# A third pair of feed-forward blocks by seven products of halves, with six weight pieces halved by DMA

## The chip, the cores and the metric

The program runs on one core of one Trainium2 chip. TensorE (PE; its weight loads are PEld) multiplies, VectorE (DVE) and ScalarE (ACT) do elementwise work, GpSimd (POOL) and SyncE (SP) issue DMAs here, and POOL computes a few small things besides. The metric is the device time of one execution in microseconds, as the median of several runs.

## The reference

Two layers on 512 tokens of 1024 channels, in fp32: a Griffin RG-LRU block, a feed-forward block (FFN), an RWKV-7 block, a second FFN, and a final RMSNorm. What matters here is the FFN, which is computed once per layer:

```
def _conv_ffn(x, norm, w_up, conv_w, conv_b, w_down):
    h = _rmsnorm(x, norm)
    u = jnp.einsum('btd,df->btf', h, w_up)
    gate = _causal_dwconv(u[..., :D_FF], conv_w, conv_b)
    hid = jax.nn.gelu(gate, approximate=True) * u[..., D_FF:]
    return jnp.einsum('btf,fd->btd', hid, w_down)
```

`D_FF` is 3072, so `w_up` is 1024 x 6144 and `w_down` 3072 x 1024; the causal convolution runs over three tokens.

## The kernel before, in words

**Precision by halves.** Every fp32 operand of a large product is written as a sum of two parts in the type that the profile calls fp32r: the rounded value (high half) and what is left (low half). `mm3` (line 81 is its matmul) issues three matmuls for one product: high x high, high x low, low x high.

**Pieces of weights.** All weights lie in DRAM as pieces of 128 x 1024 fp32 (512 KB). `plan_weights` writes their order down once, as a list. `weights_load(upto)` issues the loads of the list up to a place, `weights_split(upto)` makes the halves: ACT copies the piece into the high half (line 123), DVE subtracts (line 127). `next_weights(ahead)` loads and splits some pieces ahead of the one that it hands out. Pieces in the set `self.rounded` go another way: a DMA on POOL's queue casts the piece straight from DRAM into the high half (line 201), ACT writes its negative (line 228), and a second DMA on POOL's queue adds the piece from DRAM to that (line 229). So DVE does nothing for such a piece, and DRAM is read twice. In the kernel before these are 12 pieces of the RWKV block. All other plain loads are on SP's queue (line 206).

**The pool of buffers.** Raw pieces, halves, the normalized input `xs` and its copies `xm` share one pool of 24 buffers of 4 KB per partition (tag `b4`, `N4 = 24`). A buffer that is not free holds up the load or the copy that wants it. A planner orders each engine's instructions: it takes, in program order, what is ready by its own cost estimates, so a split or a load may stand well ahead of the place in the code that asks for it. Inside one engine the order is then fixed.

**The FFN.** The 24 blocks of 128 gate channels and 24 blocks of 128 up channels are taken as 12 pairs `n` (two gate blocks and two up blocks each). There are two ways to compute a pair:

- `Whole`: four pieces, named G0, U0, G1, U1 (gate or up, first or second 512 input channels), each 24 matmuls of 512 columns. After G1, DVE scales the gate into `gpad`, and `gate` makes convolution (ACT line 733, DVE line 735) and gelu (ACT line 736). After U1, DVE and ACT make the hidden block and its halves.
- `Halves`: input channels, tokens and gate/up are each cut in two, and the 2 x 2 products are made with seven products instead of eight, in Strassen's manner. Each product is 24 matmuls of 256 columns. They are numbered and ordered `(1, 2, 6, 5, 7), (3, 4)`, with accumulators A, D, A, F, A, F, A. Five pieces are loaded, named by the product that they first serve (f5, f1, f2, f7, f4); f5 and f7 get a second piece added by a DMA on POOL's queue (line 213). The weights of product 6 are f1 + f5, summed by DVE (line 782). Those of product 3 are that sum plus another piece, added by a POOL DMA (line 799) once the halves of product 6 are made. The halves of all seven are made by ACT and DVE on line 789. Products 1, 6 and 7 are copied out by ACT (line 817); DVE adds the rest (lines 825 to 837).

In the kernel before, pairs 0, 1 and 2 are `Whole` and pairs 3 to 11 are `Halves` (`HALVES = range(3, 12)`). The sequence of the first three pairs holds only products up; between products 7 and 3 of every later pair, and after its product 4, stands one piece of the product down, 24 matmuls of 512 columns.

**What the halves need first.** `operands()` forms the summed inputs of products 4 to 7 (tiles `xt`): 16 scaled sums and 16 low halves on DVE (lines 658 to 673), and copies on ACT. The generator `moved()`, stepped by `next(moving)`, copies parts of `xs` into `xm` with 24 ACT copies (line 693), after which products 1, 2 and 3 read `xm`; six of the 24 matmuls of product 1 go on reading `xs`. Its four steps copy 4, 4, 8 and 8 parts.

**Looking ahead in the FFN.** `products(upto, more)` goes through the sequence of (pair, product). Before each product it asks `ahead` for the weights of the next `more` products. `weights(p)` of a `Halves` pair makes the halves; for a `Whole` pair `next_weights` does it.

**The norm.** While pair 0 runs, PE makes the sums of squares (`ssq`, after G0) and later spreads the inverse root over the partitions (`rbc`, line 376, after U0); between them POOL raises to the power -0.5 (`rs`, line 372). In the second layer PE also transposes `x` into token order between the pieces of pairs 0 and 1 (`xtk`, line 627).

Of the kernel before, what the change touches and what calls it, by code (L numbers as in the profile page):

```python
# [27 lines left out]
N4 = 24  # L28
WARM = 23

HALVES = range(3, 12)

PARAMS = [
    [("lru_b_in", 16), ("lru_conv_w", 32), ("lru_conv_b", 8),
# [10 lines left out]
def pieces():  # L45

    def full(name, lead, groups):
        for g in groups:
            for k in range(0, 8, 2):
                yield name, lead, k * P, g * 512, 2  # L50

    yield from full("lru_w_in", (0,), [2, 3, 0, 1])
    yield from full("lru_w_out", (0,), [0, 1])
    for i in (1, 0):
        yield from full("rwkv_w_rkv", (0, i), [0, 1])
    for g in range(4):
        for k in range(0, 8, 4):
            yield "rwkv_w_rkv", (0, 2), k * P, g * 256, 4
    for h in range(2):
        for g in range(4):  # L60
            yield "rwkv_w_out", (0,), h * 512, g * 256, 4
    for l in range(2):
        for n in range(12):
            for j in range(2):
                for i in range(2):
                    yield "ffn_w_up", (l,), j * 512, (1 - i) * DFF + n * 256, 4
        for k in range(0, FB, 2):
            for g in range(2):
                yield "ffn_w_down", (l,), k * P, g * 512, 2


class Kernel:
# [62 lines left out]
    def plan_weights(self):  # L135
        I = self.I
        plan = []
        self.quads = {}

        index = {key: i for i, key in enumerate(pieces())}  # L140

        def piece(w, r0, c0, k):
            return I["weights"][index[w + (r0, c0, k)]].rearrange("p (k c) -> p k c", k=k)

        def add(w, r0, c0, k=2):
            plan.append((piece(w, r0, c0, k), k, False, None))

        def full(w, groups, rows=8):
            for g in groups:
                for k in range(0, rows, 2):  # L150
                    add(w, k * P, g * 512)

        def ffn(l):
            up, dn = ("ffn_w_up", (l,)), ("ffn_w_down", (l,))

            def gu(n):
                self.quads[l, n] = len(plan)
                a = lambda i, j: piece(up, j * 512, (1 - i) * DFF + n * 256, 4)
                if n in HALVES:
                    for first, more in (((1, 1), (1, 0)), ((0, 0), None), ((0, 1), None), ((1, 0), (0, 0)), ((1, 1), None)):  # L160
                        plan.append((a(*first), 4, True, more and a(*more)))
                else:
                    for i, j in ((1, 0), (0, 0), (1, 1), (0, 1)):
                        plan.append((a(i, j), 4, False, None))

            def dd(row, n, groups):
                for g in groups:
                    for k in range(0, n, 2):
                        add(dn, row + k * P, g * 512)

            for n in range(12):
                gu(n)
                if 3 <= n < 11:
                    dd((n - 3) // 2 * 512, 4, ((n - 3) % 2,))
            dd(2048, 8, (0, 1))

        full(("lru_w_in", (0,)), [2, 3, 0, 1])
        full(("lru_w_out", (0,)), [0, 1])
        ffn(0)
        r0 = len(plan) + 8  # L180
        for i in (1, 0):
            full(("rwkv_w_rkv", (0, i)), [0, 1])
        for g in range(4):
            for k in range(0, 8, 4):
                add(("rwkv_w_rkv", (0, 2)), k * P, g * 256, 4)
        self.rounded = range(r0, r0 + 12)
        for h in range(2):
            for g in range(4):
                add(("rwkv_w_out", (0,)), h * 512, g * 256, 4)
        ffn(1)  # L190
        self.plan = plan
        self.loaded, self.splitted = {}, {}
        self.n_load = self.n_split = self.n_used = 0
# [49 lines left out]
    def next_weights(self, ahead=2):  # L243
        while self.plan[self.n_used][2]:
            self.n_used += 1
        i = self.n_used
        self.weights_load(i + (3 if ahead < 3 else ahead + 2))
        self.weights_split(i + ahead)
        self.n_used += 1
        return self.splitted.pop(i)  # L250
# [355 lines left out]
    def ffn(self, l, xs, finish, after=None):  # L606
        nc, tc = self.nc, self.tc
        last = l == 1
        with tc.tile_pool(name=f"ffn{l}", bufs=1) as pool:
# [21 lines left out]
            def start(c):  # L631
                if c == 0:
                    norm.append(self.norm_end(rbs))
                    next(norm[0])
                elif c == 1:
                    next(norm[0])
                    if last:
                        self.push(by_tokens())
# [208 lines left out]
            quads = [self.quads[l, n] for n in range(12)]  # L847
            pairs, hids = {}, []
            kind = lambda n: Halves if n in HALVES else Whole
            seq = [(n, p) for n in range(12) for part in kind(n).order for p in part]  # L850
            made, at, cap = [0], [0], [len(seq)]

            def ahead(j):
                while made[0] < min(j, cap[0]):
                    n, p = seq[made[0]]
                    if n not in pairs:
                        pairs[n] = kind(n)(n)
                    pairs[n].weights(p)
                    made[0] += 1

            def products(upto, more=2):

                while True:
                    n, p = seq[at[0]]
                    at[0] += 1
                    ahead(at[0] + more)
                    pairs[n].product(p)
                    if p == "G0" and n == 2:
                        self.weights_load(quads[n + 1] + 4)
                    if n == 0 and p in ("G0", "U0"):  # L870
                        start(int(p == "U0"))
                    if n == 1 and p == "U0":
                        op.update(operands())
                    if (n, p) in ((1, "G1"), (1, "U1"), (2, "U0"), (2, "G1")):
                        next(moving)
                    if p == 5:
                        self.weights_split(quads[n] + 7)
                    if (n, p) == upto:
                        return
# [56 lines left out]
            def room(b):  # L936
                if b % 2 == 0:
                    rooms.append(pool.tile([P, 2, 2, T], F32R, tag="xt", name="hx", bufs=4))
                return rooms[-1][:, b % 2, 0], rooms[-1][:, b % 2, 1]

            products((2, "U1"))
            for n in range(3, 12):
                cap[0] = seq.index((n, 7)) + 1
                products((n, 7))
                cap[0] = seq.index((n, 4)) + 1
                ahead(at[0] + 2)
                if n < 11:
                    self.weights_load(quads[n + 1] + 2)

                def between():  # L950
                    cap[0] = len(seq)
                    if n < 11:
                        self.weights_load(quads[n + 1] + 4)
                    products((n, 4))
                    if n < 11:
                        ahead(at[0] + 3)
                        held.append(pairs[n + 1].sum)
                    elif not last:
                        self.push(self.lora_weights())

                if n < 11:
                    down((n - 3) % 2, (n - 3) // 2 * 4, 4, between)
                    ahead(at[0] + 2)
                    continue
                if not last:
                    self.norm_begin()
                down(0, 16, 8, between)
                down(1, 16, 8)
# [110 lines left out]
    @staticmethod  # L1079
    def bytok(t):  # L1080
        return t.rearrange("p (c q t) -> p c q t", q=2, t=C)
# [127 lines left out]
    def rwkv_krv(self, pool, mk, mr, AR, BK, PC, selk, LTs):  # L1209
# [95 lines left out]
        def ev_r(b, ps):  # L1305
            self.need(("r", b))
            rr = self.outer(AR, b)
            nc.vector.tensor_tensor(rr, bytok(ps), rr, ALU.mult)

        def trail(i, out, counts):  # L1310
            gen = self.mixes(i, out)
            return lambda c: [next(gen, None) for _ in range(counts[c])]

        self.push(prepare(0))
        mv = []
        self.project(mk, lambda o, ps: nc.scalar.copy(self.outer(BK, 4 + o), bytok(ps)), after=trail(0, mr, (0, 0, 2, 2)), rate=1.2, ahead=3)
        self.push(prepare(1))
        self.push(self.solve(0, AR, BK, LTs), 1)
        self.project(mr, lambda o, ps: ev_r(o, ps), rate=0.4, rate1=1.2, ahead=3)
        self.project(mr, lambda o, ps: ev_r(4 + o, ps), after=trail(2, mv, (4, 2, 2, 2)), rate=1.3, rate1=0.9, ahead=3)  # L1320
        self.tasks[0].extend(self.tasks[1])
        self.tasks[1].clear()
        return mv
# [568 lines left out]
```

## Time and profile before

| | |
|---|---|
| median of 3 runs | 1250.02 us (1249.42 to 1250.54) |
| the profiled execution | 1250.2 us, span 1248.5 us, granted clock 0.997 |
| PE busy | 1225.5 us, 98% of the span |
| DVE, ACT, POOL busy | 963.7, 678.8, 147.7 us |
| first FFN, pairs 0 to 2 | from 153.2 to 220.4 us |
| second FFN, pairs 0 to 2 | from 867.2 to 938.2 us |

Times in rows of the profile are in us from the start of the span. In the rows of a timeline or of the chain the first number is the start, the second the duration; `x24` means that 24 instructions were merged into the row; a bracket gives the idle time before and what ended it. In rows by line, the numbers after the bar are the busy time of the group in us and the mean of one in ns. Matmuls overlap in the pipeline, so the pitch from one row's start to the next is what a product costs, not the duration of one matmul.

### The profile page before, as it was taken

To read this page: it belongs to the slowest core of one execution; us is meant where nothing else is said; L and a number is where in the kernel's file an instruction comes from. 1 tells how busy PE (TensorE), PEld (TensorE's weight loads), DVE (VectorE), ACT (ScalarE), POOL (GpSimd) and SP (SyncE) were. 2 spreads that over 40 slices of the span, in tenths; PEclk is the share of its full clock that TensorE was granted. 3 is DMA by queue.
4 is the path that set the end of the run, shared out by engine and by line. 5 is a ranking of instruction groups with operands and counts; after the bars stand their busy time and mean duration, and the time that the engine had idled before them with its cause. 6 is when DMAs were issued, how large, how long until landed. Compare 5 with 4: busy or idle time off the path is not lost.

```text
span 1248.5 us, 23681 instructions
## 1 busy us (share of the span) xinstructions
PE 1225.5 (98%) x9795; PEld 1068.2 (86%) x9795; DVE 963.7 (77%) x1453; ACT 678.8 (54%) x1074; POOL 147.7 (12%) x234
## 2 busy tenths in 40 slices
PE   9999999999999999999999998999999999999997
PEld 7777888999999998878679887778889999999986
DVE  7988686777777776989898957678766777777764
ACT  6697465444444444668755356445754444444442
POOL 0000000000100000020233145310000001000000
PEclk9999999999999999999999999999999999999999
DMA  6322233666666664511566122022337666666631
GB/s 261 102 68 85 96 100 92 181 174 170 169 173 177 176 199 143 177 59 62 113 155 164 36 64 87 29 86 86 101 85 186 170 169 169 173 175 178 197 122 69
DMA packets 49389, 164.60 MB, mean 132 GB/s; under 512 B 6304, under 2 KB 8608, under 8 KB 49152
## 3 DMA queue, kind: packets, MB, share of 16 engines
q1 hardware_dynamic: 37040, 120.08, 28.1%
q0 software_dynamic: 11376, 41.42, 17.6%
q8 instruction: 77, 1.26, 0.4%
q10 hardware_dynamic: 864, 1.57, 0.4%
q14 instruction: 32, 0.26, 0.1%
HBM read 158.53 MB, written 4.52 MB: 131 GB/s over the span
## 4 chain that ended last, share of the span: by engine, by line
PE 43%; DVE 5%; ACT 3%; issue 1%; POOL 0%; POOLq 0%; DVEq 0%; ACTq 0%
PE accA L81 8%; PE acc L81 5%; PE accF L81 4%; PE acc L908 3%; PE acc L907 3%; PE acc L909 3%; PE accU L81 3%; PE accG L81 3%; PE accD L81 2%; DVE X L1391 1%; PE s L1505 1%; DVE DA L1389 1%; PE acc L1337 1%; PE pe L1549 1%; PE pd L1587 1%
## 5 line engine op out<-in xcount | busy, mean ns | idle before, releaser
L789 DVE TENSOR_TENSOR lo<-raw,hi 128x1024 fp32r<-128x1024 f32 x126 | 152.2, 1219 | 27.6 <-ACT hi L789 13.3
L127 DVE TENSOR_TENSOR wl<-raw,wh 128x1024 fp32r<-128x1024 f32 (+1 forms) x117 | 140.7, 1210 | 28.5 <-ACT wh L123 25.4
L81 PE MATMUL accA<-xt,hi 128*128 128x256 f32 x864 | 149.8, 276 | 0.0
L789 ACT CAST hi<-raw 128x1024 fp32r<-128x1024 f32 x126 | 129.4, 1047 | 34.0 <-PE acc L908 12.6
L81 PEld LDWEIGHTS accA<-xt,hi 128*128 128x128 f32 x864 | 130.2, 188 | 0.0
L123 ACT CAST wh<-raw 128x1024 fp32r<-128x1024 f32 (+1 forms) x116 | 119.2, 1044 | 18.7 <-PE accU L81 6.9
L81 PE MATMUL accA<-xt,lo 128*128 128x256 f32 x432 | 119.3, 276 | 0.0
L81 PE MATMUL acc<-hid,wh 128*128 128x512 f32 x384 | 118.2, 390 | 0.0
L817 ACT COPY s<-accA 128x512 f32<-128x512 f32 x54 | 31.7, 588 | 144.4 <-PE accA L81 144.4
L733 ACT ACTIVATE cv<-gpad,pv 128x512 f32<-128x512 f32 x48 | 37.2, 811 | 96.6 <-DVE gpad L837 93.2
L81 PEld LDWEIGHTS acc<-hid,wh 128*128 128x128 f32 x384 | 70.2, 188 | 13.1
L81 PEld LDWEIGHTS accA<-xt,lo 128*128 128x128 f32 x432 | 81.2, 188 | 0.0
L81 PE MATMUL acc<-xs,wh 128*128 128x512 f32 x248 | 77.8, 395 | 1.1 <-ACT wh L123 1.1
L213 POOL DMA_DIRECT2D raw<-in_weights_dram x36 | 31.6, 877 | 383.6 <-DMA raw<-in_weights_dram 267.6
L908 PE MATMUL acc<-wh,hid 128*128 128x512 f32 (+1 forms) x200 | 76.3, 381 | 0.0
L907 PE MATMUL acc<-wh,hid 128*128 128x512 f32 (+1 forms) x200 | 76.2, 381 | 0.0
L909 PE MATMUL acc<-wl,hid 128*128 128x512 f32 (+1 forms) x200 | 76.2, 381 | 0.0
L81 PE MATMUL acc<-hid,wl 128*128 128x512 f32 x192 | 74.5, 390 | 0.0
L735 DVE SCALAR_TENSOR_TENSOR cv<-gpad,pv,cv 128x512 f32<-128x512 f32 x96 | 67.2, 747 | 4.4 <-ACT cv L733 4.3
L81 PE MATMUL accU<-xs,wh 128*128 128x512 f32 x192 | 59.8, 392 | 0.0
L81 PE MATMUL accG<-xs,wh 128*128 128x512 f32 x192 | 59.7, 392 | 0.0
L81 PE MATMUL acc<-mix,wh 128*128 128x512 f32 x192 | 59.7, 392 | 0.0
(387 smaller groups left out, 3206.6 us busy)
## 6 DMA issues: line engine op xcount, KB each, us to landing
raw<-in_weights_dram SPq DMA_DIRECT2D x205, 512.0 KB, 4.4
raw<-in_weights_dram POOLq DMA_DIRECT2D x54, 512.0 KB, 5.6
wh<-in_weights_dram POOLq DMA_DIRECT2D x12, 512.0 KB, 6.5
wl<-in_weights_dram POOLq DMA_DIRECT2D x12, 512.0 KB, 7.0
xd<-x SPq DMA_DIRECT2D x8, 256.0 KB, 2.1
AR<-xd SPq DMA_DIRECT2D x1, 2048.0 KB, 8.6
x<-in_xT_dram SPq DMA_DIRECT2D x3, 512.0 KB, 7.0
out_dram<-xtok ACTq DMA_DIRECT2D x4, 256.0 KB, 2.1
```

The costliest lines, as they stand in the source:

```text
L81: mm = lambda *a, **kw: self.nc.tensor.matmul(ps, *a, skip_group_check=more, **kw)
L123: put = (self.nc.vector.tensor_copy if dve else self.nc.scalar.copy)(hi, src)
L127: rest = self.nc.vector.tensor_tensor(lo, src, hi.bitcast(F32), ALU.subtract)
L213: self.nc.gpsimd.dma_start(raw, more, accum_op=ALU.add)
L733: nc.scalar.activation(cv, pair.gp[:, e, 0:T], AF.Identity, bias=self.vec(f"ffn_conv_b{l}", fb), scale=cw(0))
L735: nc.vector.scalar_tensor_tensor(cv, pair.gp[:, e, j : j + T], cw(j), cv, ALU.mult, ALU.add)
L789: pair.at[p] = nc.scalar.copy(hi, f[p]), tt(lo, f[p], hi.bitcast(F32), ALU.subtract)
L817: copied = nc.scalar.copy(s[p], bank["A"])
L907: nc.tensor.matmul(ps, hh[:, s], wh[:, k, m], start=kk == 0, stop=False)
L908: nc.tensor.matmul(ps, hl[:, s], wh[:, k, m], start=False, stop=False)
L909: nc.tensor.matmul(ps, hh[:, s], wl[:, k, m], start=False, stop=kk == blocks - 1)
L1337: nc.tensor.matmul(ps, hh[:, s], wh[:, k, :], start=kk + b % 2 == 0, stop=False)
```

## The change

Pair 2 becomes a `Halves` pair too (`HALVES = range(2, 12)`). It has no piece of the product down between its products. In each layer the pieces G1 and U1 of pair 0 and all four of pair 1 join the set `self.rounded`. `next_weights` looks one piece further ahead where such a piece is near. The call of `operands()` moves from after U0 to after G0 of pair 1. The four steps of `moved()` move from pairs 1 and 2 (`Whole`) to after the products 1, 2, 3 and 4 of pair 2. The first loads of a `Halves` pair are asked for after G0 of pair 1 (for pair 2) and after product 7 of pair 2 (for pair 3). The argument `ahead=3` goes from two projections whose pieces are all in the set and so get 3 in `next_weights`.

```
-HALVES = range(3, 12)
+HALVES = range(2, 12)
...
-        self.rounded = range(r0, r0 + 12)
+        self.rounded = set(range(r0, r0 + 12))
...
         ffn(1)
+        for l in range(2):
+            self.rounded.update(range(self.quads[l, 0] + 2, self.quads[l, 2]))
...
         i = self.n_used
+        if i + 2 in self.rounded:
+            ahead = max(ahead, 3)
         self.weights_load(i + (3 if ahead < 3 else ahead + 2))
...
                     pairs[n].product(p)
-                    if p == "G0" and n == 2:
+                    if p == "G0" and n == 1:
                         self.weights_load(quads[n + 1] + 4)
...
-                    if n == 1 and p == "U0":
+                    if n == 1 and p == "G0":
                         op.update(operands())
-                    if (n, p) in ((1, "G1"), (1, "U1"), (2, "U0"), (2, "G1")):
+                    if (n, p) in ((2, 1), (2, 2), (2, 3), (2, 4)):
                         next(moving)
...
-            products((2, "U1"))
+            products((1, "U1"))
+            products((2, 7))
+            self.weights_load(quads[3] + 4)
+            products((2, 4))
+            ahead(at[0] + 2)
             for n in range(3, 12):
...
-        self.project(mr, lambda o, ps: ev_r(o, ps), rate=0.4, rate1=1.2, ahead=3)
-        self.project(mr, lambda o, ps: ev_r(4 + o, ps), after=trail(2, mv, (4, 2, 2, 2)), rate=1.3, rate1=0.9, ahead=3)
+        self.project(mr, lambda o, ps: ev_r(o, ps), rate=0.4, rate1=1.2)
+        self.project(mr, lambda o, ps: ev_r(4 + o, ps), after=trail(2, mv, (4, 2, 2, 2)), rate=1.3, rate1=0.9)
```

## The prediction, made before the run

> **What bounds the kernel now.** I read the page first, then the chain of waits in order of time, then stretches of the two FFNs.
>
> ```profile
> span 1248.5 us, 23681 instructions
> PE 1225.5 (98%) x9795; PEld 1068.2 (86%) x9795; DVE 963.7 (77%) x1453; ACT 678.8 (54%) x1074; POOL 147.7 (12%) x234
> PE 43%; DVE 5%; ACT 3%; issue 1%; POOL 0%; POOLq 0%; DVEq 0%; ACTq 0%
> ```
>
> ```profile
> 932.93 5.44 PE accU L81 x24
> 938.37 2.77 PE accA L81 x24
> 941.14 2.72 PE accD L81 x24
> 943.86 2.72 PE accA L81 x24
> 946.58 2.72 PE accF L81 x24
> 949.30 2.72 PE accA L81 x24
> 957.48 2.83 PE accF L81 x24
> 960.30 2.83 PE accA L81 x24
> 968.57 2.77 PE accA L81 x24
> ```
>
> The chain passes here through PE alone, each piece starting where the last ends: a `Whole` piece takes 5.44 us, a product of halves 2.72 to 2.83. Between 949.30 + 2.72 and 957.48 runs the piece down (5.46 us), which stands between products 7 and 3; another stands after product 4.
>
> ```profile
> 153.20:220.40 67.20, 67.20 (x306) 55.88 (x305) 51.36 (x86) 41.10 (x77) 3.88 (x3) 1.00 0.36 102
> 867.20:938.20 71.00, 71.00 (x337) 58.94 (x337) 50.69 (x84) 46.10 (x87) 3.75 (x3) 1.00 0.32 89
> 250.50:280.60 30.10, 30.10 (x218) 28.14 (x217) 22.93 (x30) 13.50 (x19) 2.61 (x3) 1.00 0.66 175
> 600.00:640.00 40.00, 37.67 (x279) 29.23 (x279) 36.00 (x71) 27.38 (x55) 11.30 (x14) 1.00 0.69 159
> ```
>
> In these rows of stretches stand length, then busy us of PE, PEld, DVE, ACT, POOL, the clock, the share of the DMA engines, GB/s. Pairs 0 to 2 (first two rows) have PE busy throughout and DVE 76 and 71%; a later pair (third row) has PE full and DVE 76%. So PE is the bound in both FFNs. Whatever shortens its stream is gained in full, unless a new wait opens.
>
> **The change, part by part.** *Pair 2.* A `Whole` pair is 4 x 5.44 = 21.76 us. Seven products are 2.77 + 4 x 2.72 + 2 x 2.83 = 19.31 if pair 2 is like the first pair of halves above, with pair 3 unchanged. Gain: 2.45 us a layer, 4.9 in both. If pair 2 takes over the slow places of products 3 and 4, and pair 3 gets 2.72 in their stead, it is 2.67 a layer, 5.3 in both.
>
> ```profile
> L81 PE MATMUL accA<-xs,hi 128*128 128x256 f32 x72 | 13.6, 282 | 0.0
> L81 PE MATMUL accA<-xm,hi 128*128 128x256 f32 x216 | 38.0, 277 | 0.0
> L123 ACT CAST wh<-raw 128x1024 fp32r<-128x1024 f32 x115 | 118.6, 1048 | 18.1 <-PE accU L81 6.9 <-PE acc L81 5.1 <-DMA raw<-in_weights_dram 4.4
> L228 ACT ACTIVATE wl<-wh 128x1024 fp32r<-128x1024 f32 x12 | 12.3, 1053 | 0.2
> L789 DVE TENSOR_TENSOR lo<-raw,hi 128x1024 fp32r<-128x1024 f32 x126 | 152.2, 1219 | 27.6 <-ACT hi L789 13.3 <-PE accU L81 12.7 <-PE acc L81 0.8
> L735 DVE SCALAR_TENSOR_TENSOR cv<-gpad,pv,cv 128x512 f32<-128x512 f32 x96 | 67.2, 747 | 4.4 <-ACT cv L733 4.3
> L830 DVE TENSOR_TENSOR s<-s,accF 128x512 f32<-128x512 f32 x18 | 12.4, 688 | 52.2 <-ACT s L817 52.2
> L693 ACT CAST xm<-xs 128x256 fp32r<-128x256 f32 x48 | 16.5, 402 | 5.4 <-PE accG L81 4.1 <-DVE wl L127 0.7 <-PE accU L81 0.4
> ```
>
> *Where pair 2 reads.* Its products 1, 2 and 3 run before the steps of `moved()`, so 66 more matmuls a layer read `xs` instead of `xm`. Product 1, with six matmuls on `xs`, is 0.05 us over product 2: 8 ns each, 0.53 a layer; the means by line differ by 5 ns. Between 0 and 0.53 I take 0.3: 0.6 in both. So PE's work falls by about 4.3 us. What is left are waits.
>
> *DVE and ACT.* Six subtractions of 1.22 us (7.3) leave DVE; ACT's six copies of 1.05 become six negations of the same length. Pair 2 costs DVE seven subtractions and a sum (9.8), four of line 735 (3.0) and some eleven of 0.69 (7.6): 20.3 us, against 4.9 + 3.0 + 8 x 0.69 = 13.4 for a `Whole` pair. So DVE's total hardly changes (+6.9 - 7.3), but 20.3 us now stand inside 19.3 us of PE. ACT gets seven copies for four, and the 24 copies of `moved()` (9.7 us) fall inside pair 2; in the first two stretches it has 25 us free.
>
> *The rounded pieces.* SP loses six loads of plain kind a layer, POOL gains twelve.
>
> ```profile
> raw<-in_weights_dram SPq DMA_DIRECT2D x205, 512.0 KB, 4.4
> L229 POOL DMA_DIRECT2D wl<-in_weights_dram x12: 866/899/1588, 597.3 to 665.6; - x12
> DMA to landing us min/median/max: 5.3/7.0/12.6
> PE rec L1289 <- DVE n L1285: 1.7, 2, 1.5
> 155.63 4.83 ACT L123 CAST wh<-raw 128x1024 fp32r<-128x1024 f32 x5
> 159.84 1.94 POOL L372 TENSOR_TENSOR rs<-ms,mhalf 128x4 f32<-128x4 f32 x1 [132.42 <-DVE ms L366]
> 165.01 1.05 PE L376 MATMUL rbc<-ident,rs 128*128 128x128 f32 x8
> 165.81 0.71 PE L81 MATMUL accG<-xs,wh 128*128 128x512 f32 x2
> ```
>
> The second and third rows are the adding DMA of the 12 pieces rounded already: 0.9 us of POOL's time, landing after 5.3 to 12.6. PE's waits from 580 to 700 us, where those are used, have no DMA among them (the fourth row is the longest). The tightest place is the first such piece, G1 of pair 0. ACT's five copies stand at 155.63; the first is U0's, the second G1's, so its negation ends near 157.6. Landing then comes at 163 to 170, by the median at 164.7; G1 starts at 165.81 and needs its low half 0.46 us later. Wait: 0 to 4 us a layer; nothing is to be won, since PE has no gap there. I take 0.2, near the median. Behind that wait on PE stand all later pieces, so each us counts. POOL's power (line 372) now has up to three issues ahead of it, 2.7 us; PE wants it at 165.01 and it ends at 161.78, so 3.2 us cover it and I cost it at nothing. Without the cover it costs what it is late. Pair 2's own first loads, asked for after G0 of pair 1, put two more additions on POOL, each held until its raw piece lands (4.4 us); behind them may stand the additions for pair 1's last pieces, which PE wants two or three pieces (10.9 to 16.3 us) later, so that is covered.
>
> The Trainium skill, "DMA: Bandwidth & Descriptors", section "Anatomy of one DMA", puts a POOL DMA at 2.0 us plus its bytes over 436 GB/s, an estimate of 3.2 us here. By that the wait above could not arise, and my first rival's chance would fall to nearly nothing; the 7.0 of the trace decides against it.
>
> *The earlier sums.* `operands()` must be done before product 6.
>
> ```profile
> 177.62 0.48 DVE L667 SCALAR_TENSOR_TENSOR s<-x,pv,s 128x256 f32<-128x256 f32 x1
> 193.35 0.75 DVE L658 TENSOR_TENSOR xt<-s,xt 128x256 fp32r<-128x256 f32 x2
> ...
> 209.03 1.23 DVE L789 TENSOR_TENSOR lo<-raw,hi 128x1024 fp32r<-128x1024 f32 x1 [5.84 <-PE accU L81]
> ```
>
> Its DVE work runs from 177.62 to 194.1 in the first layer. It is asked for one piece (5.44 us) earlier now and meets fewer subtractions, so it should end between 188 and 194. Pair 2 starts near 198.6 (one `Whole` pair before 220.33, below) and its product 6 near 204.1. Before that DVE has the evacuation of pair 1 (3.0 + 8 x 0.69 = 8.5) and two subtractions, the sum and a third (4.9): 13.4 us in 10 to 16. Late by 0 to 3.4; I take 0.1. DVE's idle 5.84 us before 209.03 are at pair 2 itself, so work can be drawn forward there.
>
> *The weights of product 3.* Here the piece down is missing as cover.
>
> ```profile
> 220.33 0.40 PE L81 MATMUL accA<-xs,hi 128*128 128x256 f32 x2
> 222.12 1.23 DVE L789 TENSOR_TENSOR lo<-raw,hi 128x1024 fp32r<-128x1024 f32 x1
> 223.64 0.87 POOL L799 DMA_DIRECT2D raw<-in_weights_dram  x1 [24.67 <-DVE lo L789]
> DMA to landing us min/median/max: 5.2/5.5/8.6
> ```
>
> In pair 3 now, product 1 starts at 220.33, the halves of product 6 end at 223.35, and POOL issues the addition at 223.64. With 5.2 to 8.6 us to land (the last row, all 18 of line 799) and 1.05 + 1.22 for the halves, product 3 could start 10.8 to 14.2 us after product 1. It is due there after 957.48 - 938.37 = 19.11 us now, in pair 2 after 2.77 + 4 x 2.72 = 13.65. So a slack of at least 4.9 falls to between 2.8 and -0.6, and DVE being late adds to it. A wait of 0 to 0.6; I take 0.2 a layer, since most of the 18 land near 5.5.
>
> *The turn to pair 3.* Its loads are asked for after product 7 of pair 2, 5.5 us before pair 3 instead of three whole pieces. SP gets four issues there; the two additions on POOL wait for their raw pieces (4.4 us), with the addition for pair 3's product 3 behind them. DVE has the gate of pair 2 (3.0 + 4 x 0.69) in the same us as pair 3's first splits. Nobody needs that gate before the piece down after pair 3's product 7, so it can slide; I take 0.1 a layer, between 0 and the 5.44 of the missing piece. The removed `ahead=3` changes no instruction: those pieces get 3 from the set.
>
> *Sum.* -4.9 + 0.6 + 2 x (0.2 + 0.1 + 0.2 + 0.1) = -3.1. The profiled execution of 1250.2 us (1.7 over its span) gives 1247.1; the median 1250.02 is 0.2 lower, so 1246.9.
>
> **The rivals.** *No change: late landings.* If the additions for G1 land after 10 us instead of 7, PE waits about 1.4 us a layer there, and with them the largest wait above, 0.6, at product 3: 4.0 in all, and 1249.9. For it: several POOL DMAs stand close together, as in the stretch from 600 us, where the DMA share is 0.69 and the longest landing 12.6. Against it: no wait of PE on a DMA there.
>
> *Slower: DVE becomes the bound.* From the start of `operands()` at 177.62 to pair 3's product 6, near 223.4, DVE has 45.8 us. It has 3.4 left of pair 0 (five of 0.69), 13.6 of sums (16 of 0.48, 16 of 0.37), 8.5 of pair 1, 20.3 of pair 2 and 4.9 of pair 3's first splits: 50.7. Unless the sums start earlier or the gate of pair 2 (5.8) slides, PE waits 4.9 us a layer. Price at 4 a layer: -4.3 + 8 = +3.7, 1253.9. It decides for slower by over 0.2% from 3.4 a layer. Against it: the idle DVE time before 209.03 and the earlier start, which together are worth more than 4.9.
>
> *Slower still: POOL starved.* If POOL could issue only while DVE rests, 24% of the first stretch, 0.9 us would become 3.7, and two issues a piece 7.5 where PE takes 5.44: 2.1 us x 6 a layer, 25 in both, 1271. The 0.9 us stand where DVE is busy 36.00 of 40 us, which would make them 9; that speaks against it. The Trainium skill, "SBUF — State Buffer", section "SBUF: two separate sides", has this rule: VectorE in a two-port mode locks GpSimd out of writing descriptors. By that row the trace does not agree for this kernel's subtractions.
>
> **How the numbers follow.** About 0.2%, 2.5 us, is what a measurement of this kernel can tell from no change. Forecast, losses under 2: 0.55, at 1244.7 to 1247.5. Late landings: 0.27, 1247.5 to 1252.5. DVE bound: 0.16, 1252.5 to 1256. POOL starved: 0.02. Faster 0.55, same 0.27, slower 0.18. The range from 1244.6 to 1252.6 leaves out the last two.
>
> **What would show it.** PE rows of 2.72 to 2.83 for seven products at pair 2 in both layers, close on one another; G1 of pair 0 starting right behind `rbc`; no waits of PE on `wl`, `lo` or a DMA between pair 0 and pair 3. The prediction is wrong if PE's gaps in that stretch exceed 2.4 us in all, or if matmuls on `xs` cost more than 8 ns extra.

## The result and the profile after

| | before | after |
|---|---|---|
| median, runs taken together | 1249.64 us (1248.76 to 1250.54) | 1257.85 us (1256.76 to 1259.55) |
| ratio, 95% interval | | 1.0069 [1.0059, 1.0079] |
| the profiled execution | 1250.2 us, span 1248.5 | 1256.76 us, span 1255.1 |

The change costs 8.2 us by the medians. A gain of 3.1 was forecast, and the range ended at 1252.6. The profiled executions are 6.6 us apart, since after's is the shortest of its six and before's is over its median. From after's page, span and busy time:

```profile
span 1255.1 us, 24039 instructions
PE 1223.2 (97%) x9939; PEld 1071.7 (85%) x9939; DVE 961.5 (77%) x1455; ACT 685.5 (55%) x1086; POOL 170.8 (14%) x264
```

PE has 2.3 us less to do than the 1225.5 of before, and the span is 6.6 longer: the loss is waiting. Lines after 190 of the kernel stand 2 to 8 further down in after than in before. The three longest lines of PE's waits in after (sum in us, times, longest):

```profile
PE accA L81 <- ACT s L821: 5.1, 3, 2.0
PE accF L81 <- DVE s L834: 2.8, 2, 1.4
PE accG L81 <- DMA wl<-in_weights_dram: 2.7, 1, 2.7
```

None of the three is among the waits of before. Where they stand is seen in stretches (columns as in the prediction), first three of before, then the same work in after: in the first FFN pairs 2 and 3; in the second pairs 0 and 1, then 2 and 3.

```profile
198.60:250.50 51.90, 51.90 (x313) 46.31 (x312) 35.95 (x44) 27.54 (x44) 2.98 (x4) 1.00 0.50 122
867.20:916.40 49.20, 49.20 (x241) 40.91 (x241) 38.69 (x69) 34.20 (x63) 3.40 (x3) 1.00 0.40 118
916.40:968.40 52.00, 52.00 (x313) 46.35 (x313) 32.36 (x37) 27.00 (x42) 2.93 (x4) 1.00 0.49 122
```

```profile
198.60:254.80 56.20, 51.04 (x386) 48.50 (x385) 44.88 (x60) 33.49 (x56) 4.34 (x5) 1.00 0.65 173
869.20:922.00 52.80, 49.80 (x241) 40.89 (x240) 33.86 (x65) 34.26 (x63) 11.72 (x13) 1.00 0.72 170
922.00:975.00 53.00, 50.28 (x385) 48.01 (x384) 35.92 (x43) 30.71 (x49) 4.37 (x5) 1.00 0.64 169
```

Read the first two numbers of a row against each other: before, PE is busy for the whole of each stretch; after, it rests for 56.20 - 51.04 = 5.2, 3.0 and 2.7 us. The stretches grow by 4.3, 3.6 and 1.0 us, 8.9 together; pairs 0 and 1 of the first FFN keep their length. Between the FFNs 2.3 us come back (250.5 to 867.2 is 616.7, 254.8 to 869.2 is 614.4), which the last experiment looks at. 8.9 - 2.3 = 6.6.

**The wait for a landing.** The chain of after in order of time passes through it, at G1 of pair 0 in the second FFN:

```profile
875.88 0.50 POOL rs L376
876.38 1.43 issue
877.81 0.23 POOL wh L203
878.04 0.36 issue
878.40 7.86 DMA wl<-in_weights_dram
...
886.30 2.59 PE accG L81 x10
```

POOL first raises the mean square to its power (`rs`, 1.96 us), for which it has waited for DVE's `ms`; then it issues a load, and only then the adding DMA of G1, which takes 7.86 us to land. ACT's negation for it had ended near 874.5.

**The wait for a gate.** Before product 6 of pair 3, the same chain:

```profile
946.36 2.66 DVE cv L739 x4
...
949.05 0.63 ACT ge L740
949.67 0.48 ACT s L821
...
950.20 3.01 PE accA L81 x24
```

Product 6 goes on in accumulator A. Line 821 must first copy product 1 out of it, and line 827, `behind(copied, pairs[pair.n - 1].bent)`, puts that copy behind the last gelu of the gate before, here pair 2's.

**The wait for a bank.** From the timelines of DVE, ACT and PE of after, before product 3 of pair 2:

```profile
936.16 0.58 ACT L821 COPY s<-accA 128x512 f32<-128x512 f32 x1 [2.07 <-PE accA L81]
936.78 0.69 DVE L834 TENSOR_TENSOR s<-s,accF 128x512 f32<-128x512 f32 x1 [1.43 <-ACT s L821]
937.52 0.51 PE L81 MATMUL accF<-xs,hi 128*128 128x256 f32 x2 [1.40 <-DVE s L834]
```

Product 3 goes on in accumulator F, where product 5 was. DVE has to read it there, for which it first needs ACT's copy of product 7. In every other pair the piece down runs on PE meanwhile.

**Late sums in the first FFN.** Timelines of ACT, DVE and PE of after:

```profile
172.80 1.06 ACT L230 ACTIVATE wl<-wh 128x1024 fp32r<-128x1024 f32 x1 [4.59 <-DMA wh<-in_weights_dram]
174.60 1.54 DVE L739 SCALAR_TENSOR_TENSOR cv<-gpad,pv,cv 128x512 f32<-128x512 f32 x2 [4.92 <-ACT cv L737]
182.76 0.47 DVE L671 SCALAR_TENSOR_TENSOR s<-x,pv,s 128x256 f32<-128x256 f32 x1
204.04 0.68 DVE L771 TENSOR_TENSOR s<-s,ge 128x512 f32<-128x512 f32 x1
204.76 0.62 ACT L123 CAST hid<-s 128x512 fp32r<-128x512 f32 x1 [1.27 <-DVE s L771]
205.95 0.57 ACT L821 COPY s<-accA 128x512 f32<-128x512 f32 x1
206.57 0.50 PE L81 MATMUL accA<-xt,hi 128*128 128x256 f32 x2 [2.03 <-ACT s L821]
```

ACT works in order: a negation waits 4.59 us for its rounded piece, the gate's first step behind it on ACT is held, and DVE is idle for 4.92 us. The sums start at 182.76, 5.1 later than the 177.62 of before, though they are asked for earlier; pair 1's evacuation ends late, and product 6 of pair 2 waits.

### The profile page after: what moved, and what is told of

It is laid out like the page before. It is cut to its first block, busy times and chain, and to the rows that moved or that the text cites. A ratio compares the mean times of both kernels' runs of the same rounds, so it can differ in the third digit from the quotient of the medians.

```text
span 1255.1 us, 24039 instructions
## 1 busy us (share of the span) xinstructions
PE 1223.2 (97%) x9939; PEld 1071.7 (85%) x9939; DVE 961.5 (77%) x1455; ACT 685.5 (55%) x1086; POOL 170.8 (14%) x264
## 4 chain that ended last, share of the span: by engine, by line
PE 39%; DVE 6%; ACT 4%; issue 3%; POOL 1%; DMA 1%; POOLq 0%; DVEq 0%; ACTq 0%
PE accA L81 8%; PE accF L81 4%; PE acc L81 4%; PE acc L912 3%; PE acc L911 3%; PE acc L913 3%; PE accD L81 2%; PE accU L81 1%; PE accG L81 1%; DVE X L1399 1%; PE s L1513 1%; DVE DA L1397 1%; PE acc L1345 1%; PE acc L1346 1%; PE acc L1347 1%
## 5 line engine op out<-in xcount | busy, mean ns | idle before, releaser
L793 DVE TENSOR_TENSOR lo<-raw,hi 128x1024 fp32r<-128x1024 f32 x140 | 168.8, 1218 | 18.3 <-ACT hi L793 18.2
L81 PE MATMUL accA<-xt,hi 128*128 128x256 f32 x960 | 167.1, 277 | 5.1 <-ACT s L821 5.1
L793 ACT CAST hi<-raw 128x1024 fp32r<-128x1024 f32 x140 | 143.4, 1046 | 36.9 <-PE acc L912 12.6
L81 PEld LDWEIGHTS accA<-xt,hi 128*128 128x128 f32 x960 | 144.7, 188 | 5.7 <-ACT s L821 5.7
L81 PE MATMUL accA<-xt,lo 128*128 128x256 f32 x480 | 132.7, 276 | 0.0
L127 DVE TENSOR_TENSOR wl<-raw,wh 128x1024 fp32r<-128x1024 f32 (+1 forms) x97 | 116.7, 1208 | 12.5 <-ACT wh L123 9.8
L123 ACT CAST wh<-raw 128x1024 fp32r<-128x1024 f32 (+1 forms) x96 | 99.2, 1043 | 7.1 <-PE acc L81 5.2
L81 PEld LDWEIGHTS accA<-xt,lo 128*128 128x128 f32 x480 | 90.2, 188 | 0.0
L834 DVE TENSOR_TENSOR s<-s,accF 128x512 f32<-128x512 f32 x20 | 13.7, 687 | 61.6 <-ACT s L821 61.6
L81 PEld LDWEIGHTS acc<-xs,wh 128*128 128x128 f32 x248 | 45.9, 188 | 13.3 <-issue 2.4
```

What stands on the lines that cost most here:

```text
L81: mm = lambda *a, **kw: self.nc.tensor.matmul(ps, *a, skip_group_check=more, **kw)
L123: put = (self.nc.vector.tensor_copy if dve else self.nc.scalar.copy)(hi, src)
L127: rest = self.nc.vector.tensor_tensor(lo, src, hi.bitcast(F32), ALU.subtract)
L793: pair.at[p] = nc.scalar.copy(hi, f[p]), tt(lo, f[p], hi.bitcast(F32), ALU.subtract)
L834: tt(s[7], s[7], bank["F"], ALU.add)
```

## The experiments

Two theories after that comparison. ORDER: the waits come from the order written into pairs 2 and 3 (the tie of line 827 and the shared bank F). LANDING: they come from the rounded pieces, whose DMAs land late and hold ACT, DVE and PE. The first three kernels take one thing each out of after; the fourth has the rounding alone.

**e1: the tie.**

```
-                            behind(copied, pairs[pair.n - 1].bent)
+                            if pair.n not in (2, 3):
+                                behind(copied, pairs[pair.n - 1].bent)
```

> The changed kernel, but in pairs 2 and 3 the copy of product 1 is no longer tied behind the gelu of the pair before. Theory ORDER: PE's waits inside pairs 2 and 3 come from the order that is written into those pairs, which the piece down used to cover. Then the waits before product 6 of pair 3 (1.9 us in the first layer, 1.5 in the second) go, and that before product 6 of pair 2 in the first layer (2.35) shrinks by about 0.6, since the copy still stands behind other ACT work there: 4.0 us less than the changed kernel, 1253.9. Theory LANDING: the waits follow from rounded pieces that land late and hold ACT and DVE up; the tie is only where the lateness shows, and the waits reappear one product later: at most 1 us less, 1257 or more.

Measured: 1254.47 us (1252.77 to 1256.7), ratio to before 1.0038 [1.0024, 1.0053]: 3.4 less than after. PE's waits:

```profile
PE accG L81 <- DMA wl<-in_weights_dram: 3.6, 1, 3.6
PE accF L81 <- DVE s L835: 3.0, 2, 1.6
```

The line on accumulator A has fallen from 5.1 us to 0.9, which is at product 6 of pair 2 in the first FFN; the two others stand. ORDER's 1253.9 was close; 0.8 us come back in product 7 of pair 3, which waits for `lo`.

**e2: a bank for product 3 of pair 2.**

```
-                    name = {1: "A", 5: "F", 2: "D"}.get(p)
+                    name = {1: "A", 5: "F", 2: "D", 3: "H" if pair.n == 2 else None}.get(p)
...
+                        if pair.n == 2:
+                            tt(s[6], s[6], bank["F"], ALU.add)
...
-                        later(tt(s[6], s[6], bank["F"], ALU.add), pair.n + 1, 1)
+                        later(tt(s[6], s[6], bank["H" if pair.n == 2 else "F"], ALU.add), pair.n + 1, 1)
```

> The changed kernel, but product 3 of pair 2 gets an accumulator of its own instead of going on in that of product 5, and DVE adds it in one more instruction of 0.69 us. ORDER: product 3 waits (1.67 and 1.56 us) because DVE must read accumulator F first, after ACT's copy of product 7 (0.59) and an addition (0.69), with no piece down between; these 3.2 us go, some 0.3 come back from the extra addition: 1255.0. LANDING: DVE reads late because it is behind; the same lateness then shows at product 4 or at pair 3: at most 1 us less.

Measured: 1255.01 us (1252.7 to 1258.01), ratio 1.0045 [1.0027, 1.0063]: 2.8 less than after. That is ORDER's number, but with four executions that spread over 5.3 us so close a hit is partly luck. What the trace shows is that the line on accumulator F is gone and the two others stand:

```profile
PE accA L81 <- ACT s L821: 4.5, 3, 1.8
PE accG L81 <- DMA wl<-in_weights_dram: 2.7, 1, 2.7
```

**e3: no rounded piece in the FFNs.** The pair by halves as in after, the two added lines on `self.rounded` taken out, so that ACT and DVE split these pieces again.

> The changed kernel, but the six pieces of each layer are loaded and halved in the old way (SP, ACT, DVE), none by casting DMA. ORDER: only the wait at G1 of pair 0 in the second layer (2.9 us and 0.7 beside it) goes, 3.6 less; the 5.7 before product 6 and the 3.2 before product 3 stay: 1254.3. If the six subtractions (7.3 us a layer) make DVE the bound in pair 2, up to 5 us a layer come back: 1259 to 1264. LANDING: besides the 3.6, the sums start earlier and the wait of 2.35 before product 6 in the first layer and half of the others go: about 1250.

Measured: 1249.93 us (1249.56 to 1251.86), ratio 1.0004 [0.9995, 1.0014]: 7.9 less than after. Its waits, and from DVE's timeline the first sum:

```profile
PE accF L81 <- DVE s L832: 2.8, 2, 1.4
...
PE accA L81 <- ACT s L819: 2.3, 2, 1.3
```

```profile
177.91 0.47 DVE L669 SCALAR_TENSOR_TENSOR s<-x,pv,s 128x256 f32<-128x256 f32 x1
```

The wait for the landing is gone, product 6 of pair 2 no longer waits, and the sums start at 177.91 instead of 182.76, although DVE has 13.6 us more to do (975.1 busy against 961.5). So DVE was not short of time in after: it was held. The waits of the tie (pair 3) and the bank stay.

**e4: the rounding alone.** The kernel before, with the six rounded pieces a layer and the look-ahead in `next_weights`, without the halves.

> The kernel before with the six pieces of each layer rounded by DMA and the look-ahead that goes with them, and nothing else: pair 2 stays whole. Both theories: G1 of pair 0 waits some 3 us in the second layer as in the changed kernel, 0 to 1 in the first, and DVE's saved subtractions win nothing, since PE is the bound: 1249.6 + 3.5 = 1253. ORDER: no other wait opens. LANDING: further waits of 1 us or more open at pairs 1 to 3, 1255 or more.

Measured: 1253.72 us (1251.74 to 1254.99), ratio 1.0033 [1.0022, 1.0044]: 4.1 over before. The wait is there again:

```profile
PE accG L81 <- DMA wl<-in_weights_dram: 2.3, 1, 2.3
```

In the first FFN it costs nothing visible (pair 4 starts at 250.53, as before); in the second, pairs 0 and 1 take 54.0 us instead of 49.2. No further wait opens at pairs 1 to 3, so that e4 comes out as ORDER had it (1253) and not as LANDING had it (1255 or more). LANDING's number was met in e3 (1250), ORDER's in e1 and e2. So both theories hold in part, each for its own waits, and the rounding takes 4.1 us by itself but 7.9 in the change: there it also makes the sums late, which pair 2 by halves wants earlier. The next four kernels have both edits of e1 and e2.

**e5: both edits, rounding kept.**

> The changed kernel with both edits to the order of the work (the first products of pairs 2 and 3 no longer tied behind the gate before them; product 3 of pair 2 in a bank of its own), the rounded pieces kept. SEPARATE (the waits of the order and of the landings stand at different places, so that their prices add): 1257.85 - 3.4 - 2.85 = 1251.6, PE's row lengths before products 3 and 6 at 2.72 to 2.9 in both layers, and layer 1's wait for G1's low half still 2.9 to 3.6 us. SHARED (they stand in for one another: DVE is late anyway, and a wait that goes opens the next): 1253.5 or more, with a new wait of PE on DVE inside pairs 2 or 3.

Measured: 1250.35 us (1248.94 to 1251.45), ratio 1.0007 [0.9998, 1.0016]: 7.5 less than after, where the two edits alone add up to 6.2.

```profile
PE accG L81 <- DMA wl<-in_weights_dram: 2.6, 1, 2.6
...
PE accA L81 <- ACT s L821: 1.2, 1, 1.2
```

What is left are the two waits of the rounding. SEPARATE holds; the 1.3 us beyond the sum are within the spread of e2's executions.

**e6: both edits, no rounding in the FFNs.**

> Both edits to the order, and no rounded piece in the FFNs (three DVE subtractions a layer and FFN come back for every three rounded pieces, six in each layer). What the halves alone are worth: 1249.9 of the kernel without rounding, less its waits before product 3 (1.7 and 1.56) and product 6 of pair 3 (1.2 and 1.5), 6.0 in all, gives 1243.9; with a few tenths for the added sum and DVE's extra work 1244 to 1245.5. Should DVE be the bound of pairs 2 and 3 instead, the waits come back elsewhere: 1247 or more.

Measured: 1244.11 us (1244.06 to 1245.45), ratio 0.9961 [0.9948, 0.9973]: 5.3 under before. In its stretches (the same three pieces of work) PE rests for 1.2 us in the first and not at all in the others, with DVE at 975.9 us in all:

```profile
198.40:249.60 51.20, 50.03 (x385) 47.81 (x384) 42.93 (x53) 34.50 (x59) 5.20 (x6) 1.00 0.72 191
864.10:913.40 49.30, 49.30 (x242) 40.95 (x241) 40.13 (x71) 33.98 (x63) 4.59 (x4) 1.00 0.42 98
913.40:963.10 49.70, 49.70 (x386) 47.82 (x385) 36.69 (x44) 30.94 (x49) 4.29 (x5) 1.00 0.70 190
```

```profile
PE accA L81 <- DVE lo L791: 1.2, 1, 1.2
```

The last line is that rest: in the first FFN product 6 of pair 3 waits for its low half, which DVE makes behind the convolution of pair 2's gate. So DVE costs 1.2 us there and nothing else in these stretches.

**e7: both edits, only the four pieces of pair 1 rounded.** It asks whether the rounding costs by its transfers as such or by the first pieces.

```
-            self.rounded.update(range(self.quads[l, 0] + 2, self.quads[l, 2]))
+            self.rounded.update(range(self.quads[l, 1], self.quads[l, 2]))
```

> As the kernel with both edits to the order and all six rounded pieces a layer, but only the four pieces of pair 1 rounded; the last two of pair 0 are split by ACT and DVE again. FIRST PIECE (what costs is that G1 of pair 0 is wanted so soon): no wait for G1 in layer 1, sums in layer 0 on time, 1244 to 1246.5. BURST (what costs is that so many long transfers of POOL's queue land one after another, whichever they are): the wait moves to pair 1's pieces, with 1 to 3 us a layer, 1248 to 1251.

Measured: 1244.47 us (1244.38 to 1245.09), ratio 0.9961 [0.9949, 0.9974]. FIRST PIECE. Its adding DMA, its first two stretches and its wait:

```profile
DMA to landing us min/median/max: 5.4/8.8/12.8
```

```profile
198.60:248.90 50.30, 50.15 (x386) 47.84 (x385) 40.61 (x51) 30.79 (x52) 4.25 (x5) 1.00 0.73 185
863.30:912.60 49.30, 49.30 (x242) 40.93 (x241) 34.97 (x65) 33.64 (x62) 10.29 (x12) 1.00 0.66 163
```

```profile
PE accA L81 <- DVE lo L793: 0.2, 1, 0.2
```

The additions land as slowly as ever (after has 5.3/8.0/13.8 in this row), but PE wants these pieces later, and nobody waits: the last line, what is left of e6's 1.2, is all that PE waits for from pair 0 to pair 3.

**e8: the root left out.** In the second FFN (layer 1 in the expectation) POOL's order had the power of the norm ahead of G1's addition. A constant takes its place here, on DVE, in both FFNs.

```
...
-        nc.gpsimd.tensor_tensor(rs, ms, self.mhalf.to_broadcast([P, 4]), ALU.pow)
+        nc.vector.tensor_scalar(rs, ms, 0.0, 0.25, ALU.mult, ALU.add) if self.in_ffn else nc.gpsimd.tensor_tensor(...)
...
```

> As the kernel with both edits to the order and all six rounded pieces, but the inverse root of the FFNs' norm (1.96 us on POOL) is left out: VectorE writes a constant in its place (0.2 us), after the same wait for the mean square. PE, ACT and SP have the same instructions in the same order. QUEUE (in layer 1 the adding DMA of G1 stands behind the root in POOL's order, which waits for the mean square): it is issued near 874.5 instead of 878.4 of the changed kernel's clock, lands 3 to 4 us earlier, PE's wait there falls from 2.9-3.6 to under 0.7, and the time is about 2.9 under that of the kernel with the root, 1248.7 if that has 1251.6. BURST (the transfers in flight hold it up, wherever it stands): it is issued earlier and lands at nearly the same time; time within 0.7 of the kernel with the root. In layer 0, where the addition stands ahead of the root, neither expects a change.

Measured: 1245.41 us (1245.25 to 1247.12), ratio 0.9972 [0.9962, 0.9983]: 4.9 under e5, where 2.9 was expected. POOL's timeline of e5, then of e8:

```profile
871.29 1.96 POOL L376 TENSOR_TENSOR rs<-ms,mhalf 128x4 f32<-128x4 f32 x1 [22.00 <-DVE ms L370]
873.22 0.59 POOL L203 DMA_DIRECT2D wh<-in_weights_dram  x1
873.81 1.88 POOL L231 DMA_DIRECT2D wl<-in_weights_dram  x2
```

```profile
870.31 1.85 POOL L231 DMA_DIRECT2D wl<-in_weights_dram  x2 [15.80 <-ACT wl L230]
```

And the chain at the place where after's ran through the DMA, in e5, then in e8:

```profile
881.58 4.15 PE accG L81 x10
```

```profile
877.59 0.67 PE rbc L380 x6
878.26 2.30 PE accG L81 x10
```

The addition now waits for ACT's negation alone, is issued 3.5 us and lands 4.7 us earlier, and PE runs from `rbc` straight into G1. Pairs 0 and 1 of the second FFN fall from 54.3 us (864.60 to 918.86) to 49.3 (864.41 to 913.69). QUEUE holds, BURST doesn't: the transfers behind the first land just as late as in e5 (10 to 15 us after issue). About 0.5 of the 5.0 us is the root's own time, since e5's `rbc` waits 0.5 longer for `rs`, and 2.8 are the wait for the landing. The other 1.6, which QUEUE's 2.9 had not counted, come from the pace behind that wait: from 881.9 to 885.3 us e5's granted clock is 0.50, and G1's first ten matmuls take 3.99 us to the start of the next work, against 2.39 in e8. The wait of 1.2 in the first FFN stays (1.0 in e8), where the addition stood ahead of the root anyway.

**e9: eight matmuls more at the start of the kernel before.** Every kernel with pair 2 by halves is 2.3 us shorter between the FFNs, whatever else it has. What is missing there is a stop of PE, in before's timeline the second row here (e4 has it too, with 1.3 us). Behind it the granted clock of before is 0.54 from 779.5 to 783 us, where e4 has 1.00:

```profile
776.54 0.45 PE L1587 MATMUL pd<-tu 128*64 128x64 f32 x8 [0.30 <-ACT tu L1581]
778.68 0.45 PE L1587 MATMUL pd<-tu 128*64 128x64 f32 x8 [1.70 <-issue]
```

```
-WARM = 23
+WARM = 31
```

> The kernel before with 31 matmuls instead of 23 on the identity at the very start, so that everything behind stands eight matmuls later in PE's stream. It looks for the 1.7 us in which PE waits for nothing that the profile shows, in the kernel before in the middle of the sixteen matmuls of line 1587 near 778.7, the 6201st matmul of PE; it is there with the six rounded pieces alone (1.3 us, the same matmul of PE) and in no kernel with pair 2 by halves, whose stream has 72 matmuls more ahead of that place. STREAM (it belongs to a position in PE's stream): it stays at about the 6201st matmul, which is now one of line 1549 or 1587 eight earlier, or it is gone. PLACE (it belongs to this work, by something the profile does not show): it stays in the middle of line 1587's matmuls, now the 6209th, with 1.3 to 1.7 us. The time is some tenths of a us to 1.5 over that of before for the eight matmuls (0.19 us each), by either.

Measured, with one execution of each: 1249.32 us, beside 1249.47 of before. The same sixteen matmuls in its timeline:

```profile
777.34 0.69 PE L1587 MATMUL pd<-tu 128*64 128x64 f32 x16 [1.54 <-ACT tu L1521]
```

The stop has moved eight matmuls forward in the work, to the head of the sixteen: the same place, the 6202nd by the trace (the expectation's 6201st), in PE's stream. The granted clock behind it is low here too, 0.56 in the same window. Here the profile gives ACT as what ended it, so part of the 1.54 may be that wait. This speaks for STREAM, on the strength of a single run. So of the 5 us that e6 and e7 win, up to 2.3, the stop and the low clock behind it, belong to the length of PE's stream ahead of that place and not to cheaper work.

## Why the prediction was wrong, by its own steps

What held: PE's work fell about as forecast (4.3). In the three stretches together PE is busy 153.1 us before, 149.0 in e6 and 149.2 in e7, 4 less; in after 151.1, and there products at and just behind a wait run slower (2.81 to 2.98 instead of 2.72 to 2.86). Reading `xs` cost 0.4 us a layer, 0.3 taken: products 1, 2 and 3 of pair 2 take 2.87, 2.88 and, in e6, 2.86. Where no wait stands, pairs 2 and 3 take 49.7 us in the second FFN; the prediction's steps give 52.0 - 2.45 + 0.3 = 49.85. The addition for product 3, its tightest transfer, was in time: PE has no wait on a DMA or on `lo` there, nor in e6 and e7, where product 3 starts without any wait.

What failed are the waits, put at 0.6 a layer, 1.2 in all. PE rests for 10.9 us in the three stretches of after; the prediction called itself wrong from 2.4. Its other sign did not come: the matmuls on `xs` cost 6 ns more (0.4 us over 66), not over 8.

- *The turn to pair 3*, 0.1 a layer. "Nobody needs that gate before the piece down after pair 3's product 7, so it can slide": line 827 needs it, and product 6 needs line 827. Measured 1.9 and 1.5 us; without the tie (e1), no wait there. The prediction had "between 0 and the 5.44 of the missing piece" as bounds and took the low end by a sentence on the data, without reading the order written out by hand. The same tie at pair 2 passed the late gate of pair 1 on to its product 6.
- *The weights of product 3*, 0.2 a layer. The step saw that the missing piece down was cover, but asked only for the weights. The bank was covered by it as well: 1.7 and 1.6 us, gone in e2.
- *The rounded pieces*, 0.2 a layer. In the first FFN G1 itself waits for nothing, as taken. In the second, pairs 0 and 1 lost 3.6. "POOL's power (line 372) now has up to three issues ahead of it" was read from the first FFN; in the second the order is the other way round, and the issues stand behind the power. What was late was not the root but what stood behind it, which e8 shows.
- *The earlier sums*, 0.1. They "should end between 188 and 194"; they started 5.1 us later than before and ended at 201.1. The step counted DVE's work and left out that DVE waits for ACT, and ACT, in order, for a landing. That chain is read from the trace; e3 and e7, which have no such hold in front of the gate, have no wait at product 6 of pair 2.

The rival *late landings* named the right transfer with half the cause (a slow landing; the late issue in front of it was missed) and at half the price, 4.0 us where the rounding took 7.9. *DVE becomes the bound* forecast waits on DVE in the right place, and its price of 4 a layer is near the 5.2 of the first FFN, but not its reason: e6 has more work on DVE and less waiting, and what DVE costs by itself is e6's 1.2 us in all. *POOL starved* is not seen: issues without a queue before them take 0.85 to 0.9 us in after as before. Whether the rule that the prediction set beside it applies to these subtractions at all, no run here shows, so the trace does not speak against it.

The 3.2 us of the Trainium skill, "DMA: Bandwidth & Descriptors", section "Anatomy of one DMA", do not agree with the adding DMA here either: 5.3 to 13.8 us in after.

## What to carry to other kernels

Where a piece of work is taken out from between two others on the bound engine, list everything that it covered: the data of the next piece, but also the evacuation of the accumulator that it will overwrite, and every order written by hand. A transfer's lateness is its landing time plus what stands ahead of its issue, so read the issuing queue's order at each place where the code runs, not at one of them; here the same code gave the opposite order in the two layers. A step that puts a wait for a DMA on an in-order engine delays the steps behind it, so prefer pieces that are wanted late (e7 against e5: 5.9 us).

## What was not expected of the hardware

POOL's DMAs of 512 KB that are issued within 3 us land one after the other: in the second FFN of after the six issued from 877.81 to 880.62 land 5.8, 7.9, 11.0, 11.8, 13.8 and 14.5 us after issue. In these bursts landing time is thus a matter of place in the burst more than of the DMA's kind, which the medians by kind (6.2 and 8.0 us in after) hide.

Behind some waits of PE the granted clock was 0.50 for 3.413 us, and behind others it stayed at 1.00. Cut each trace into windows of that length, counted from the point where the clock first reaches 1.00. Six windows in the eleven traces are followed by one at 0.50, apart from the end of the program, and they are the six in which PE rests longest: 2.0 and 2.1 us in before and e9 (the stop of the last experiment), 3.4, 2.3 and 2.6 at G1 of the second FFN in e1, e4 and e5, and 1.77 at product 6 of pair 2 in e2. No other window has more than 1.68. So in these traces the clock halves when PE has rested for more than half of a window. The 2.7 us at G1 in after are split by a window's end into 1.0 and 1.68, so after goes without, and its first ten matmuls of G1 take 2.43 us, against 3.8 to 4.0 in e1, e4 and e5. One such stretch costs about 1.7 us (an estimate, half of 3.4). The price of a wait thus depends on where it falls.

PE stopped for 1.3 to 1.7 us ahead of the 6202nd matmul of its stream in three kernels (before, e4, e9), though in the last the work there was another by eight matmuls. Why is not settled; a stop in the supply of instructions is one possibility. The Trainium skill, "Runtime: NRT & Kernel Launch", section "Instruction fetch mechanics", says that an engine's program is fetched in blocks of 256 instructions and that crossing into the next one is mostly hidden; no run here shows the fetch itself. In the kernels with halves the same position falls on other work, and no such stop is seen.
